# Four Strassen sets by turns with classical pairs in the down projection, and the last products added in DRAM by DMAs

## The chip, the cores and the metric

The kernel runs on one core of a Trainium2 chip. The metric is the device time of one execution in microseconds (us); for the kernel before, three runs gave 1673.4, 1674.53 and 1674.97 us, median 1674.53.

The engines are named as in the profile: PE (TensorE matmuls), PEld (TensorE weight loads), DVE (VectorE), ACT (ScalarE), POOL (GpSimd) and SP (SyncE). SP and POOL start most DMAs here.

## The reference

A decoder layer on 256 tokens of width 2048 in float32: a feed-forward half step, a mixer (attention beside a convolution), and a second feed-forward half step, each followed by a LayerNorm. The change lies in the down projection of the two feed-forward steps:

```python
def swiglu_ffn(x, w_gate, w_up, w_down):
    h = jax.nn.silu(x @ w_gate) * (x @ w_up)      # 256 x 5632
    return h @ w_down                             # 256 x 2048
x = layer_norm(ALPHA * x + 0.5 * swiglu_ffn(x, ...), ln_g, ln_b)
```

## The kernel before

**Two-term numbers.** Every float32 operand is split into a high part `hi` (a cast on ACT, L170) and a low part `lo` (raw minus `hi`, on DVE, L174). A product is three matmuls, hi·hi, hi·lo and lo·hi (`mm3`, L677 to L679), accumulated in PSUM.

**Parts.** The 5632 hidden features are worked in three parts, of 16, 16 and 12 blocks of 128. For each part the up projection comes first, then gate and transpose (the transposed tile goes out to DRAM and back by POOL's DMAs, L1044 and L1046), then the down projection of that part. Parts 0 and 1 project down to all 2048 columns, in two column pairs of 2 × 512 columns; their results are written or added into a DRAM tile `y` (`side`) by POOL's DMAs. Part 2 does its first two column chunks in the same way into SBUF and the rest otherwise. The two feed-forward steps so have eight column pairs that go to DRAM: four stretches ("downs") of two.

**Sets and pairs.** `by_sums` (L865) forms a 2 × 2 block product (two token halves by two column chunks) over K pairs of 256 features each. `KINDS` (L26) says for each K pair whether it is done classically ("C": 8 products, 24 matmuls, 2 weight tiles of 128 × 1024) or as a Strassen set ("S": 7 products, 21 matmuls). A set takes four weight sources out of the same two tiles `more`: DVE forms sums of them (L188, four subtractions), and the raw and summed tiles are each split. A set also needs sums of the four `hh` blocks on the left side, made when `hf` comes back (`split`, L1056).

**The eight banks.** All eight PSUM banks hold sums of one column pair: banks 1, 5, 6 and 7 of the Strassen products alone, banks 2, 4, 3 and 0 of products that belong to one output each. After the last set, `shared` (L941) combines banks 1, 5, 6 and 7 into four SBUF tiles `part` (one ACT copy, L944, and four DVE additions, L938). After the last classical pair, `leave` (L952) adds each of the banks 2, 4, 3, 0 to its `part` (DVE, L938), and POOL starts a DMA that writes `part` to `y` (L964, part 0 of the first step) or adds it there (`accum_op`, L962). The next column pair uses the same banks again, in the order 1, 5, 6, 7, 2, 4, 3.

**The order of the work** is the program's order: each engine has one queue, and takes its instructions in that order. `Steps` decides while the program is written when a weight source is split: `pace` (L279) puts in a split when its estimate of DVE's backlog is under `AHEAD` (1.2 us), at most `LEAD` (7) sources ahead of the one in use; during the last products of a column pair (`ending`) it puts in none. `hi` and `lo` have 8 buffers each, the raw tiles 4, the sets' tiles room for two sets. The tiles `part` (and others) take turns in 5 buffers of tag `z`: a new tile waits until all readers of the buffer's last tile are done, a DMA that reads it included.

Of the kernel before, what the change touches and what calls it, by code (L numbers as in the profile page):

```python
# [9 lines left out]
F32 = mybir.dt.float32  # L10
# [4 lines left out]
ALU = mybir.AluOpType  # L15
# [3 lines left out]
P = 128  # L19
# [3 lines left out]
KT = D // P  # L23
JT = DFF // P
PARTS = ((0, 16), (16, 32), (32, 44))
KINDS = ("SCCSCSCC", "SCCSCSCC", "SCCSCC")  # L26
BLOCKS = {"S": 7, "C": 4, "L": 8}
UP = (
# [35 lines left out]
ZB = 5  # L64
# [15 lines left out]
def blocks_of(columns):  # L80
    return lambda kind: BLOCKS["L" if kind == "S" and columns < NC_ else kind]
# [265 lines left out]
def hybrid_layer(  # L347
# [3 lines left out]
    nc = tc.nc  # L351
# [4 lines left out]
    act = ctx.enter_context(tc.tile_pool(name="act", bufs=1))  # L356
# [20 lines left out]
    def add_ffn(wu, wd, plain):  # L377
        for (j0, j1), kinds in zip(PARTS, KINDS):
            for g in range(j0 // JG, j1 // JG, 2):
                if g < plain:  # L380
                    sources.extend(wu[g + i, q, h] for i in range(2) for q in range(4) for h in range(2))
                else:
                    for t, kind in UP[up_of(g, j0, plain)]:
                        add_set(kind, [wu[g + i, t // 2, t % 2] for i in range(2)])
            for c in range(0, NC_, 2):
                if c > 0 and j1 == JT:
                    sources.extend(wd[c + i, t // 2, t % 2] for i in range(2) for t in range(j0 // 2, j1 // 2))
                    continue
                for t, kind in enumerate(kinds, j0 // 2):
                    add_set(kind, [wd[c + i, t // 2, t % 2] for i in range(2)])  # L390
# [290 lines left out]
    def block(x_, k, b):  # L681

        if x_.shape[2] == S:
            return x_[:, k, b * P : (b + 1) * P]
        kinds = KINDS[-1]
        return x_[:, sum(4 if y == "C" else 8 for y in kinds[: k // 2]) + 2 * (k % 2) + b]
# [235 lines left out]
    def down_by_sums(hh, hl, kinds, factor, side, more, columns, last):  # L922

        firsts = [sum(map(blocks_of(columns), kinds[:t])) for t in range(len(kinds))]
        places = {
            "S": ("21", "11", "22", "12", "S1", "S2", "S3", "S4")[-blocks_of(columns)("S"):],
            "C": ("21", "11", "22", "12"),
        }

        def blocks(t, name):  # L930
            n = firsts[t] + places[kinds[t]].index(name)
            return hh[:, n], hl[:, n]

        for c in range(0, columns, 2):
            tmp, places_ = [], {(0, 0): 0, (0, 1): 2, (1, 0): 1, (1, 1): 3}

            def add(out, ps, other):
                nc.vector.scalar_tensor_tensor(out=out, in0=ps, scalar=factor, in1=other, op0=ALU.mult, op1=ALU.add)  # L938
                st.vector(0.62, 0.3)

            def shared(bank, tmp=tmp):  # L941

                tmp.extend(act.tile([P, 512], F32, tag="z", name="part", bufs=ZB) for k in range(4))
                nc.scalar.mul(tmp[0], bank[1], factor)  # L944
                add(tmp[1], bank[6], tmp[0])
                add(tmp[2], bank[5], tmp[1])
                add(tmp[1], bank[7], tmp[1])
                add(tmp[3], bank[5], tmp[1])
                if last is not None:
                    last()  # L950

            def leave(at, ps, c=c, tmp=tmp):  # L952

                t = tmp[places_[at]]
                add(t, ps, t)
                if columns < NC_:
                    y = xts[0][:, 1 - at[0], (c + at[1]) * 512 : (c + at[1] + 1) * 512]
                    joins[1 - at[0], at[1]] = lambda: nc.vector.tensor_tensor(out=y, in0=y, in1=t, op=ALU.add)
                    return
                place = side[1 - at[0], :, (c + at[1]) * 512 : (c + at[1] + 1) * 512]  # L960
                if more:
                    nc.gpsimd.dma_start(place, t, accum_op=ALU.add)  # L962
                else:
                    nc.gpsimd.dma_start(place, t)  # L964

            by_sums(kinds, blocks, leave, shared)

    def ffn(xc, tag, skew, begun, prepare, finish, places, kept=None):
        with tc.tile_pool(name=f"ffn{tag}", bufs=2) as pool:
# [40 lines left out]

            for part, ((j0, j1), kinds) in enumerate(zip(PARTS, KINDS)):
                n = j1 - j0
# [108 lines left out]
                while g < j1 // JG:  # L1121
# [4 lines left out]
                    g += 2  # L1126
                side = sides[xc is not xcat]
                down_by_sums(
                    hh, hl, kinds, 0.5, side, part > 0 or xc is not xcat, columns, (lambda: tokens_back(side)) if ends else None
                )  # L1130
# [466 lines left out]
```

## Time and profile before

| what | value |
|---|---|
| median of three runs | 1674.53 us (1673.4 to 1674.97) |
| time of the profiled execution | 1675.41 us |
| its span, first to last instruction | 1673.6 us |
| DVE, ACT, POOL busy over the span | 1444.1 us (86%), 944.6 us (56%), 323.0 us (19%) |
| share of the DMA engines' time, SP's queue q1 and POOL's queue q0 | 56.6% and 11.1% |
| first and last matmul of the first down (stretch A) | 175.71 and 258.44 us |
| first matmul of the other downs (B, C, D) | 426.63, 1137.03 and 1387.95 us |

A row of the timeline has start, duration (of a merged run of equal instructions, "x4"), engine, line, operation, output from inputs, and in brackets the idle time before it and what ended that. A row of the windows has, for a stretch, its length and each engine's busy time (with its count of instructions), the granted TensorE clock, the share of the DMA engines and GB/s. A row of the groups has count, busy time and mean ns of one.

### The profile page before, as it was taken

Reading aid. Unit: us, or ns where it says so; the run is one execution under the profiler, and the core shown is the slowest. Engines: PE = TensorE matmul, PEld = TensorE weight load, DVE = VectorE, ACT = ScalarE, POOL = GpSimd, SP = SyncE. Lnnn points to the kernel's source line nnn. Section 1 sums busy time; section 2 is a strip of 40 time slices with the busy share of each in tenths; the row PEclk is TensorE's granted clock in tenths of the full one; section 3 lists DMA queues with packets and bytes.
Section 4 is the critical chain, followed back from the end, with each engine's and each line's share of the span. In section 5 each row is a group of like instructions: output and inputs, shape, how many; then the busy total and the mean of one; then the engine's idle time right before and its main releaser. Section 6 shows DMA issues by size and latency. Waiting matters only on the chain. (4 is left out here: it accounts for less than half of the span.)

```text
span 1673.6 us, 21985 instructions
## 1 busy us (share of the span) xinstructions
PE 1657.9 (99%) x7647; PEld 1375.4 (82%) x7647; DVE 1444.1 (86%) x2151; ACT 944.6 (56%) x1316; POOL 323.0 (19%) x302
## 2 busy tenths in 40 slices
PE   9999999999999999999999999999999999999997
PEld 7888888888878888888888888888888888888885
DVE  7899899888999987958888768799999888999877
ACT  6555555555555554676665466455555555556552
POOL 0100000111100001178996201000000000000012
PEclk9999999999999999999999999999999999999999
DMA  8667677677788666656654568666776666776665
GB/s 296 242 227 239 208 250 244 201 249 243 245 242 261 207 225 243 211 189 189 201 176 159 192 226 286 233 223 226 240 244 222 223 222 208 257 235 216 219 238 158
DMA packets 110976, 377.32 MB, mean 225 GB/s; under 512 B 13968, under 2 KB 14096, under 8 KB 110736
## 3 DMA queue, kind: packets, MB, share of 16 engines
q1 hardware_dynamic: 94032, 329.50, 56.6%
q0 software_dynamic: 16112, 45.10, 11.1%
q10 hardware_dynamic: 720, 1.31, 0.2%
q8 instruction: 60, 0.98, 0.2%
q14 instruction: 52, 0.43, 0.1%
HBM read 349.64 MB, written 27.26 MB: 225 GB/s over the span
## 5 line engine op out<-in xcount | busy, mean ns | idle before, releaser
L174 DVE TENSOR_TENSOR lo<-raw,hi 128x1024 fp32r<-128x1024 f32 x320 | 376.1, 1219 | 60.1 <-ACT hi L170 59.9
L677 PE MATMUL sum<-hi,xcat 128*128 128x512 f32 x1006 | 391.6, 389 | 0.4 <-DVE part L1077 0.4
L678 PE MATMUL sum<-lo,xcat 128*128 128x512 f32 x1006 | 391.4, 389 | 0.0
L679 PE MATMUL sum<-hi,xcat 128*128 128x512 f32 x1006 | 391.4, 389 | 0.0
L170 ACT CAST hi<-raw 128x1024 fp32r<-128x1024 f32 x320 | 321.5, 1047 | 59.2 <-DMA raw<-in_wd 19.0
L170 ACT CAST hi<-more 128x1024 fp32r<-128x1024 f32 (+1 forms) x210 | 190.6, 907 | 178.8 <-DVE more L188 158.7
L174 DVE TENSOR_TENSOR lo<-more,hi 128x1024 fp32r<-128x1024 f32 (+1 forms) x210 | 213.7, 1040 | 20.3 <-ACT hi L170 20.2
L677 PE MATMUL sum<-hi,hh 128*128 128x512 f32 x580 | 226.2, 390 | 1.3 <-DVE part L938 1.0
L678 PE MATMUL sum<-lo,hh 128*128 128x512 f32 x580 | 225.7, 389 | 0.0
L679 PE MATMUL sum<-hi,hl 128*128 128x512 f32 x580 | 225.7, 389 | 0.0
L677 PEld LDWEIGHTS sum<-hi,xcat 128*128 128x128 f32 x1006 | 188.8, 188 | 40.4 <-DVE part L1077 1.2
L679 PEld LDWEIGHTS sum<-hi,xcat 128*128 128x128 f32 x1006 | 188.8, 188 | 39.4
L678 PEld LDWEIGHTS sum<-lo,xcat 128*128 128x128 f32 x1006 | 188.8, 188 | 39.0
L253 ACT CAST hi<-raw 128x1024 fp32r<-128x1024 f32 (+1 forms) x156 | 158.5, 1029 | 93.2 <-PE acc L679 42.2
L256 POOL TENSOR_TENSOR lo<-raw,hi 128x1024 fp32r<-128x1024 f32 x73 | 175.9, 2436 | 111.6 <-ACT hi L253 104.8
L170 ACT CAST hi<-sum 128x512 fp32r<-128x512 f32 x140 | 86.8, 622 | 191.4 <-DVE sum L188 177.8
L1044 POOL DMA_DIRECT2D far<-hr x88 | 49.2, 564 | 753.0 <-DVE hr L1039 753.0
L677 PEld LDWEIGHTS sum<-hi,hh 128*128 128x128 f32 x580 | 108.8, 188 | 25.8 <-ACT hi L170 1.3
L679 PEld LDWEIGHTS sum<-hi,hl 128*128 128x128 f32 x580 | 108.9, 188 | 22.7
L678 PEld LDWEIGHTS sum<-lo,hh 128*128 128x128 f32 x580 | 108.9, 188 | 22.6 <-DVE lo L174 0.2
L1077 DVE TENSOR_TENSOR part<-sum,part 128x512 f32<-128x512 f32 x152 | 101.0, 687 | 26.8 <-PE sum L679 19.4
L256 DVE TENSOR_TENSOR lo<-raw,hi 128x1024 fp32r<-128x1024 f32 (+1 forms) x83 | 97.7, 1198 | 25.7 <-ACT hi L253 25.5
(210 smaller groups left out, 2436.1 us busy)
## 6 DMA issues: line engine op xcount, KB each, us to landing
raw<-in_wu SPq DMA_DIRECT2D x264, 512.0 KB, 5.0
raw<-in_wd SPq DMA_DIRECT2D x120, 512.0 KB, 5.3
more<-in_wu SPq DMA_DIRECT2D x84, 512.0 KB, 7.0
more<-in_wd SPq DMA_DIRECT2D x56, 512.0 KB, 7.3
raw<-in_win SPq DMA_DIRECT2D x52, 512.0 KB, 3.9
raw<-in_wout SPq DMA_DIRECT2D x32, 512.0 KB, 4.0
far<-hr POOLq DMA_DIRECT2D x88, 128.0 KB, 2.7
hf<-far POOLq DMA_DIRECT2D x22, 512.0 KB, 3.6
```

The source lines that it names most:

```text
L170: self.nc.scalar.copy(hi, x_)
L174: self.nc.vector.tensor_tensor(out=lo, in0=x_, in1=hi.bitcast(F32), op=ALU.subtract)
L253: nc.scalar.copy(hi, raw)
L256: eng.tensor_tensor(out=lo, in0=raw, in1=hi.bitcast(F32), op=ALU.subtract)
L677: nc.tensor.matmul(ps, s_hi, m_hi, start=start, stop=False)
L678: nc.tensor.matmul(ps, s_hi, m_lo, start=False, stop=False)
L679: nc.tensor.matmul(ps, s_lo, m_hi, start=False, stop=stop)
L1044: nc.gpsimd.dma_start(far[:, :, t].rearrange("f r n -> r f n"), hr[32 * t : 32 * t + 32])
L1077: nc.vector.tensor_tensor(out=out, in0=ps, in1=other, op=ALU.add)
```

## The change

Three things are changed.

1. `KINDS` of parts 0 and 1: from "SCCSCSCC" (three sets, five classical pairs) to "SCSCSCSC" (four and four). The last set is now followed by one classical pair, not two. Part 2 stays.
2. For the eight column pairs that go to DRAM, `shared` itself sends off the four `part` tiles (`write`), right after they are made.
3. `leave` no longer adds on DVE for these. ACT copies the bank, times `factor`, into a new tile `rest` of tag `z` (L972 of the new file), and POOL's DMA adds that to `y`. Each column pair so has eight DMAs of 256 KB to `y`, not four.

```diff
-KINDS = ("SCCSCSCC", "SCCSCSCC", "SCCSCC")
+KINDS = ("SCSCSCSC", "SCSCSCSC", "SCCSCC")
...
                 if last is not None:
                     last()
+                else:
+                    for at, k in places_.items():
+                        write(at, tmp[k], more)
+
+            def write(at, t, adds, c=c):
+
+                place = side[1 - at[0], :, (c + at[1]) * 512 : (c + at[1] + 1) * 512]
+                if adds:
+                    nc.gpsimd.dma_start(place, t, accum_op=ALU.add)
+                else:
+                    nc.gpsimd.dma_start(place, t)
 
             def leave(at, ps, c=c, tmp=tmp):
 
                 t = tmp[places_[at]]
-                add(t, ps, t)
                 if columns < NC_:
+                    add(t, ps, t)
...
-                place = side[1 - at[0], :, (c + at[1]) * 512 : (c + at[1] + 1) * 512]
-                if more:
-                    nc.gpsimd.dma_start(place, t, accum_op=ALU.add)
-                else:
-                    nc.gpsimd.dma_start(place, t)
+                t = act.tile([P, 512], F32, tag="z", name="rest", bufs=ZB)
+                nc.scalar.mul(t, ps, factor)
+                write(at, t, True)
```

The first place is ACT's queue around the end of the first column pair of stretch A, in the kernel before. The number behind `hi` is the weight source: sources 76 to 97 belong to this column pair, 98 to 101 are the first set of the next one. A name in "waits" is what the instruction waits for (DMAHW: a DMA of SP's queue, DMASW: one of POOL's).

```order
L170 CAST hi97_1856<-raw97_1746 128x1024 [waits DMAHW0_49,PE_49,Activation_49]
L170 CAST hi98_1877<-more_446 128x1024 [waits DMAHW1_49,PE_49,Activation_49]
L170 CAST hi99_1884<-sum99_1880 128x512 [waits DVE_49,PE_49]
L170 CAST hi99_1884<-sum99_1881 128x512 [waits DVE_49]
L944 ACTIVATE part_1892<-sum_1621 128x512
L170 CAST hi100_1917<-more_446 128x1024 [waits DVE_49,DMAHW2_49,PE_49,Activation_49]
L170 CAST hi101_1929<-more_446 128x512 [waits DVE_49,PE_49]
L170 CAST hi102_1942<-raw102_1830 128x1024 [waits DMAHW3_49,PE_49,Activation_49]
```

The same place in the changed kernel. Here the column pair has sources 76 to 99, its last set is 94 to 97 and its last classical pair 98 and 99; 100 to 103 are the first set of the next column pair.

```order
L170 CAST hi101_1916<-sum101_1913 128x512 [waits DVE_49]
L170 CAST hi102_1939<-more_446 128x1024 [waits DVE_49,DMAHW2_49,PE_49,Activation_49]
L944 ACTIVATE part_1943<-sum_1623 128x512
L972 ACTIVATE rest_1962<-sum_1626 128x512 [waits PE_49]
L972 ACTIVATE rest_1971<-sum_1627 128x512 [waits DMASW4_49,DVE_49,PE_49]
L972 ACTIVATE rest_1986<-sum_1628 128x512 [waits DMASW5_49,DVE_49,PE_49]
L972 ACTIVATE rest_1989<-sum_1628 128x512 [waits DMASW6_49,DVE_49]
L170 CAST hi103_2002<-more_446 128x512 [waits DVE_49]
L170 CAST hi104_2005<-raw104_1818 128x1024 [waits DMAHW3_49]
L170 CAST hi105_2012<-raw105_1827 128x1024 [waits DMAHW4_49]
```

The four copies `rest` stand in one row ahead of the cast of source 103. The first takes the one free buffer of tag `z`; the second, third and fourth each wait for a DMA of POOL's queue. At the end of the second column pair of each down the rows stand in the same way, with all four sources of the following set cast ahead of the copies.

POOL's queue there, in the changed kernel (L961 writes, L959 adds):

```order
L961 DMA y0_137<-part_1943 128x512 [waits Activation_49]
L961 DMA y0_137<-part_1945 128x512 [waits DVE_49]
L961 DMA y0_137<-part_1944 128x512 [waits DMASW6_49,DVE_49]
L961 DMA y0_137<-part_1946 128x512 [waits DVE_49]
L959 DMA y0_137<-rest_1962 128x512 [waits DMASW4_49,Activation_49]
L959 DMA y0_137<-rest_1971 128x512 [waits DMASW6_49,Activation_49]
L959 DMA y0_137<-rest_1986 128x512 [waits DMASW5_49,Activation_49]
L959 DMA y0_137<-rest_1989 128x512 [waits DMASW7_49,DMASW3_49,Activation_49]
```

Each addition of a `rest` waits for the DMA of the `part` that goes to the same place: DMASW4, 5 and 6 are raised by the first, second and third of these rows. The copies of ACT that wait for DMASW4, 5 and 6 so wait until these three DMAs have landed. In the kernel before there were four DMAs here, each after its `leave`.

DVE's queue around `shared`, in the changed kernel:

```order
L174 TENSOR_TENSOR lo100_1901<-more_446,hi100_1900 128x1024 [waits Activation_49]
L174 TENSOR_TENSOR lo101_1917<-sum101_1912,hi101_1916 128x512 [waits Activation_49]
L174 TENSOR_TENSOR lo101_1917<-sum101_1913,hi101_1916 128x512 [waits Activation_49]
L188 TENSOR_TENSOR more_446<-more_446 128x512
L174 TENSOR_TENSOR lo102_1940<-more_446,hi102_1939 128x1024 [waits Activation_49]
L938 SCALAR_TENSOR_TENSOR part_1944<-sum_1625,part_1943 128x512 [waits PE_49,Activation_49]
L938 SCALAR_TENSOR_TENSOR part_1945<-sum_1625,part_1944 128x512 [waits DVE_49]
L938 SCALAR_TENSOR_TENSOR part_1944<-sum_1624,part_1944 128x512 [waits DVE_49,PE_49]
L938 SCALAR_TENSOR_TENSOR part_1946<-sum_1625,part_1944 128x512 [waits DVE_49]
L188 TENSOR_TENSOR more_446<-more_446,sum101_1913 128x512
L174 TENSOR_TENSOR lo103_2003<-more_446,hi103_2002 128x512 [waits PE_49,Activation_49]
L174 TENSOR_TENSOR lo104_2006<-raw104_1818,hi104_2005 128x1024 [waits DMAHW3_49,PE_49,Activation_49]
```

Ahead of the four additions stand the low parts up to source 102; before, they stood up to source 98. The low part of 103, and all behind it, needs a cast that stands behind the four copies on ACT.

## Prediction

> **What bounds the kernel now.** I read the page first, then who waits for whom, then the two column pairs of the first down (stretch A) by windows, and then the engines' timelines at the end of a column pair.
>
> ```profile
> PE 1657.9 (99%) x7647; PEld 1375.4 (82%) x7647; DVE 1444.1 (86%) x2151; ACT 944.6 (56%) x1316; POOL 323.0 (19%) x302
> PE sum L677 <- DVE part L938: 1.0, 2, 0.9
> 175.71:217.20 41.49, 41.49 (x185) 34.36 (x184) 37.22 (x49) 22.75 (x30) 2.77 (x5) 1.00 0.60 207
> 217.20:258.70 41.50, 41.50 (x185) 34.37 (x184) 38.77 (x48) 23.48 (x28) 2.75 (x5) 1.00 0.66 232
> ```
>
> PE is never idle in a column pair of A, so a matmul less is time less. The longest entry of PE's waits in the downs is 1.0 us in all, for the additions that the change removes. But DVE is close behind: 37.2 and 38.8 us busy in 41.5. ACT has room, 23 of 41.5. So DVE has some 3 us of slack per column pair, and the change must be weighed on DVE, and on whatever keeps DVE from working.
>
> **PE: what is saved.** The first and last matmul of A:
>
> ```profile
> 175.71 0.39 PE L677 MATMUL sum<-hi,hh 128*128 128x512 f32 x1
> 258.44 0.39 PE L679 MATMUL sum<-hi,hl 128*128 128x512 f32 x1
> ```
>
> A has two column pairs of 3×21 + 5×24 = 183 matmuls, 366 in all: 82.73 / 365 = 0.2267 us each. One set in place of a classical pair saves 3 matmuls; eight column pairs save 24, **5.4 us**. A column pair then has 180 matmuls, 40.8 us. A set takes 4.76 us, a classical pair 5.44.
>
> **DVE: what is added.** One set and the two classical sources after it:
>
> ```profile
> 183.53 0.65 DVE L188 TENSOR_TENSOR sum<-more 128x512 f32<-128x512 f32 x1
> 184.21 0.69 DVE L188 TENSOR_TENSOR sum<-more,sum 128x512 f32<-128x512 f32 x1
> 184.82 0.68 DVE L188 TENSOR_TENSOR more<-more 128x512 f32<-128x512 f32 x1
> 185.43 1.22 DVE L174 TENSOR_TENSOR lo<-more,hi 128x1024 fp32r<-128x1024 f32 x1
> 186.68 0.69 DVE L188 TENSOR_TENSOR more<-more,sum 128x512 f32<-128x512 f32 x1
> 187.29 1.28 DVE L174 TENSOR_TENSOR lo<-sum,hi 128x512 fp32r<-128x512 f32 x2
> 188.49 1.82 DVE L174 TENSOR_TENSOR lo<-more,hi 128x1024 fp32r<-128x1024 f32 x2
> 190.23 2.35 DVE L174 TENSOR_TENSOR lo<-raw,hi 128x1024 fp32r<-128x1024 f32 x2
> 192.50 0.68 DVE L188 TENSOR_TENSOR sum<-more 128x512 f32<-128x512 f32 x1
> ```
>
> From start to start a set costs DVE 190.23 − 183.53 = 6.70 us and a classical pair 192.50 − 190.23 = 2.27. The swap adds 4.43. The four additions of `leave` go; at about 0.6 us from start to start, like the 512-wide rows above, that is 2.4. Net +2.0 us per column pair on DVE while PE's share falls by 0.7: slack of about 3 us becomes about none. ACT gets three casts of 512 more (a set has two of 1024 and three of 512, a classical pair two of 1024) and four copies of 0.59, 4.2 us in all; it is idle for 18 us of a column pair, so in time that has room. POOL gets four issues more, some 3.5 us beside its 2.8 of 41.5, and its next other work after a down is the transpose of the next part, tens of us later. What matters is where ACT's copies stand.
>
> **ACT: the wait that is added.** `shared` in A, on ACT and DVE, with what DVE does just ahead of it:
>
> ```profile
> 209.35 0.59 ACT L944 ACTIVATE part<-sum 128x512 f32<-128x512 f32 x1
> 248.55 0.59 ACT L944 ACTIVATE part<-sum 128x512 f32<-128x512 f32 x1
> 207.37 0.68 DVE L188 TENSOR_TENSOR sum<-more 128x512 f32<-128x512 f32 x1
> 208.09 0.69 DVE L188 TENSOR_TENSOR sum<-more,sum 128x512 f32<-128x512 f32 x1
> 208.70 1.22 DVE L174 TENSOR_TENSOR lo<-more,hi 128x1024 fp32r<-128x1024 f32 x1
> 209.97 2.94 DVE L938 SCALAR_TENSOR_TENSOR part<-sum,part 128x512 f32<-128x512 f32 x4
> ```
>
> A DMA to `y` in stretch B, from its addition on, then the landing times of the 24 adding DMAs (L962) and of the 8 plain ones (L964, in A):
>
> ```profile
> 471.12 0.68 DVE L938 SCALAR_TENSOR_TENSOR part<-sum,part 128x512 f32<-128x512 f32 x1
> 472.24 0.88 POOL L962 DMA_DIRECT2D y<-part  x1 [11.56 <-DVE part L938]
> DMA to landing us min/median/max: 5.2/7.6/9.8
> DMA to landing us min/median/max: 3.4/5.5/7.0
> ```
>
> Of the four new copies, the second to fourth wait for the first three of these DMAs to land, and behind the fourth stand ACT's casts for the next sources. Let T be the start of the copy L944. The third addition of `shared` ends about T+2.8 (0.62 to the first, three of some 0.73). POOL issues the first DMA at T+1.0, the second at T+2.5, the third 0.88 later, T+3.4. With the median of 7.6 the third lands at T+11.0; the fourth copy, 0.59, ends at **T+11.6**. For the plain ones of A, with 5.5 and an issue at T+3.1, it is T+9.2. Casts and low parts then follow at these times:
>
> ```profile
> L170 ACT CAST hi<-more 128x512 fp32r<-128x512 f32 x70 | 43.5, 622 | 70.8 <-DVE more L188 70.8
> L174 DVE TENSOR_TENSOR lo<-more,hi 128x512 fp32r<-128x512 f32 x70 | 47.9, 685 | 7.8 <-ACT hi L170 7.8
> L170 ACT CAST hi<-raw 128x1024 fp32r<-128x1024 f32 x320 | 321.5, 1047 | 59.2 <-DMA raw<-in_wd 19.0 <-DMA raw<-in_wu 17.8 <-ACT hi L170 12.2
> L174 DVE TENSOR_TENSOR lo<-raw,hi 128x1024 fp32r<-128x1024 f32 x320 | 376.1, 1219 | 60.1 <-ACT hi L170 59.9
> ```
>
> After the first column pair of a down the next source is 103: 0.62 + 0.69, ready at T+12.9 (A: 10.5). PE comes to it one classical pair and five products of the next set after its last set's end E: 5.44 + 15×0.2267 = E+8.84. After the second column pair the whole next set is ready, and the next source is classical: 1.05 + 1.22, T+13.9 (A: 11.5), wanted at E + 5.44 + 4.76 = E+10.20. With the lag T − E, PE stands still for lag + 4.1 and lag + 3.7 us (A: lag + 1.7 and + 1.3).
>
> The lag now: E is 135 matmuls, 30.60 us, after a column pair's start, so 209.35 − 206.31 = 3.0 us, and 248.55 − 247.80 = 0.75 in the second. In the changed kernel DVE has, from the start of the down to `shared`, one set more and one classical pair less (+4.4), and it has got to source 102, not 98: 5.5 us of the next set (two subtractions, one 1024-wide and two 512-wide low parts, a subtraction, a 1024-wide one) for the 2.5 of the rows above. That is +7.4, and E comes 21 matmuls later, 4.8: the lag becomes 3.0 + 7.4 − 4.8 = **5.6**. So the first stall is 9.7 us (A: 7.3). For the second: T to T takes DVE 39.2 now (209.35 to 248.55), 41.2 with the 2.0 added, and DVE lies idle behind ACT from its last addition and one subtraction, T+4.2, to the end of the cast, T+12.2, 8.0 us (A: 5.6). PE takes 40.8 and the first stall. Lag: 5.6 + 41.2 + 8.0 − 40.8 − 9.7 = 4.3 (A: 5.6 + 41.2 + 5.6 − 40.8 − 7.3 = 4.3), stall 8.0 (A: 5.6).
>
> **The sum.** Three downs at 17.7 and A at 12.9: 66.0 us of stalls. Less 5.4 for matmuls and 1.0 for the wait that goes: +59.6 on the profiled execution's 1675.41, 1735.0; that execution was 0.9 over the median, so the forecast is **1734 us**.
>
> Bounds of the unknown sizes. Lag 0.75 everywhere and the shortest landings (5.2 and 3.4, that is 2.4 and 2.1 off): stalls 2.45 + 2.05 per down in B, C and D, 0.35 in A, 14 in all, net +7, 1682. Longest landings (9.8, 7.0) with the lags above: 2.2 more per stall in three downs, 1.5 in A, +16, net +76, 1750. Not in the sum: the left side's sums for a further set, once per down, of this kind:
>
> ```profile
> L1001 DVE TENSOR_TENSOR sums<-hf 128x128 f32<-128x128 f32 x32 | 7.8, 283 | 0.0
> ```
>
> Four of 0.28 add 1.1 to the first lag of a down, 4 in all. And DVE leaves each down with no lead over PE, which the up projections before had to spare at will; a stall or two of some 3 us in each of the four that follow would add some 8 to 12, which makes 1762 of the 1750. I take the medians: 24 and 8 DMAs of the same kind, size and place.
>
> **The rivals.**
>
> *The landing is short.* While ACT waits, raw tiles aren't freed and SP loads nothing, so the DMA engines, at 0.60 to 0.70 now, may be free for these DMAs. With the shortest landing seen, 3.4, for all: third landing T+6.8, copy T+7.4, source 103 at T+8.7. Stalls lag − 0.1 = 5.5 and, with DVE's idle time 3.8, lag 5.6 + 41.2 + 3.8 − 40.8 − 5.5 = 4.3, 4.3 − 0.5 = 3.8: 9.3 a down, 37, net +31, 1705. Against it: all 24 adding DMAs took 5.2 or more, with the load as it was. [...]
>
> *DVE alone is the bound.* If the copies wait for nothing late, what is left is DVE's lag of 5.6: bank 5 is free at T+3.6 and wanted at E + 5.44 + 0.68, a stall of 3.1, then about 0.5 in the second: 14 in all, net +8, 1682. It needs landings under 3 us.
>
> *Faster.* DVE sheds 32 additions of 512 from the ends of the column pairs, where PE's only waits were, and ACT is idle for 18 us of each. If the copies are hidden, only the 5.4 and 1.0 are left: −6.4, 1668. It decides at the landing: with the smallest lag, 0.75, source 103 is in time if the third DMA lands 2.8 us after its issue (8.84 − 0.75 − 3.4 − 0.59 − 0.62 − 0.69). Of 32 DMAs none did. [...]
>
> *Not what it says.* The rows show 24 matmuls fewer, 32 additions fewer and 32 copies more; I give nothing to this.
>
> **Chances.** Forecast 0.79 (its own range 1695 to 1762); short landing 0.10 (1695 to 1715); DVE alone 0.05 (1677 to 1690); faster 0.06. A measurement of this kernel can tell about 0.2%, 3.3 us, from no change. Slower by more than that: 0.91, since of the second and third case some 0.03 ends within it; same 0.03; faster 0.06. The range for 8 in 10 leaves out the two last cases and a part of the forecast's ends: 1695 to 1762.
>
> **What would show it.** Right: on ACT, L972 idle before it with DMA `y<-part` as what ended the wait, three times per column pair; PE waiting at the first set of the next column pair for ACT or DVE (`hi`, `lo`, `rest`, `part`), 5 to 10 us each time, eight times; DVE idle some 6 to 8 us behind L170 at these places; PE busy time down by about 5 us. Wrong: PE's windows in the downs still full, or idle time in them with no L972 ahead of it; or PE waiting in the up projections instead.

## The result, and the profile after

The changed kernel takes 1744.58 us (median of four runs, 1743.28 to 1745.0); the kernel before, on the same chip, 1673.97 us. The ratio is 1.0421, interval 1.0405 to 1.0437: **4.2% slower**, 70.6 us. The profiled execution has a span of 1743.1 us, 69.5 more than the one of before.

The page's first part, then PE's and ACT's waits that bear on the downs (whole execution: total us, times, longest), and the two column pairs of A, the first up to the next one's first matmul, the second to the end of its last, in the changed kernel:

```profile
PE 1686.0 (97%) x7623; PEld 1387.7 (80%) x7623; DVE 1466.2 (84%) x2195; ACT 978.2 (56%) x1376; POOL 350.5 (20%) x334
PE sum L677 <- DVE part L938: 17.9, 8, 2.7
PE sum L677 <- ACT part L944: 8.4, 8, 2.9
PE sum L677 <- ACT hi L170: 7.6, 3, 3.4
PE sum L678 <- DVE lo L174: 6.5, 9, 1.3
PE sum L677 <- ACT rest L972: 4.1, 3, 1.9
ACT rest L972 <- DMA y<-part: 56.7, 24, 5.0
175.46:217.96 42.50, 41.27 (x181) 33.52 (x179) 38.24 (x54) 23.27 (x32) 2.77 (x5) 1.00 0.54 191
217.96:264.87 46.91, 44.25 (x180) 35.74 (x180) 39.43 (x50) 25.21 (x32) 5.76 (x8) 0.93 0.75 224
```

There are 24 matmuls fewer, and PE is busy 28.1 us longer. The second window tells why: the granted clock is 0.93 there. Who waits is also not what one would guess from ACT's 56.7 us of waiting for landings: PE's two longest entries, 26.3 us together, name the additions L938 and the copy L944 of `shared`, which wait for no landing themselves. PE's timeline at the end of the first column pair of A shows how these lie:

```profile
217.18 0.39 PE L679 MATMUL sum<-hi,hl 128*128 128x512 f32 x1
217.96 0.50 PE L677 MATMUL sum<-hi,hh 128*128 128x512 f32 x1 [0.39 <-ACT part L944]
...
218.54 0.39 PE L679 MATMUL sum<-hi,hl 128*128 128x512 f32 x1
221.58 0.80 PE L677 MATMUL sum<-hi,hh 128*128 128x512 f32 x1 [2.65 <-DVE part L938]
...
222.60 0.63 PE L679 MATMUL sum<-hi,hl 128*128 128x512 f32 x1
...
227.96 0.39 PE L677 MATMUL sum<-hi,hh 128*128 128x512 f32 x1
```

PE stops at the first product of the next column pair (bank 1), three matmuls later at the second (bank 5), and then runs for some 6 us with 0.43 us from start to start where 0.227 is its pace; the granted clock from 221.58 to 227.60 is 0.50. ACT and DVE in the same place:

```profile
216.37 1.05 ACT L170 CAST hi<-more 128x1024 fp32r<-128x1024 f32 x1 [2.44 <-DVE more L188]
217.32 0.59 ACT L944 ACTIVATE part<-sum 128x512 f32<-128x512 f32 x1
217.81 0.59 ACT L972 ACTIVATE rest<-sum 128x512 f32<-128x512 f32 x1
221.09 0.60 ACT L972 ACTIVATE rest<-sum 128x512 f32<-128x512 f32 x1 [2.69 <-DMA y<-part]
223.25 0.60 ACT L972 ACTIVATE rest<-sum 128x512 f32<-128x512 f32 x1 [1.57 <-DMA y<-part]
224.37 0.60 ACT L972 ACTIVATE rest<-sum 128x512 f32<-128x512 f32 x1 [0.52 <-DMA y<-part]
```

```profile
217.45 1.23 DVE L174 TENSOR_TENSOR lo<-more,hi 128x1024 fp32r<-128x1024 f32 x1 [1.25 <-ACT hi L170]
218.59 2.93 DVE L938 SCALAR_TENSOR_TENSOR part<-sum,part 128x512 f32<-128x512 f32 x4
...
225.50 0.69 DVE L174 TENSOR_TENSOR lo<-more,hi 128x512 fp32r<-128x512 f32 x1 [3.38 <-ACT hi L170]
```

The three waits for landings are there, with ACT's casts behind them and DVE idle for 3.38 us; but PE's stop at bank 5 ends at 221.58, with DVE's four additions, before any of that reaches PE.

I counted PE's starts against its pace of 0.227 from start to start, over all products of the projections (tile `sum`). Stops with a named wait cost 50.8 us, in 31 places (before: 2.0, in 3). Matmuls at half clock, which start 0.38 to 0.46 after the one before, cost 21.3 us, and there are 107 (before: none). Other starts more than 0.30 after the one before cost 7.1 (before: 2.3). Less 5.4 us for the 24 matmuls that is +69.5, all of the span's growth. The same count comes within 1.4 us of the span's growth in every run below.

### The profile page after: what moved, and what is told of

It is laid out like the page before. It is cut to its first block, busy times and chain, and to the rows that moved or that the text cites. A ratio compares the mean times of both kernels' runs of the same rounds, so it can differ in the third digit from the quotient of the medians.

```text
span 1743.1 us, 22118 instructions
## 1 busy us (share of the span) xinstructions
PE 1686.0 (97%) x7623; PEld 1387.7 (80%) x7623; DVE 1466.2 (84%) x2195; ACT 978.2 (56%) x1376; POOL 350.5 (20%) x334
## 3 DMA queue, kind: packets, MB, share of 16 engines
q0 software_dynamic: 20720, 53.49, 14.3%
## 5 line engine op out<-in xcount | busy, mean ns | idle before, releaser
L174 DVE TENSOR_TENSOR lo<-raw,hi 128x1024 fp32r<-128x1024 f32 x304 | 357.5, 1220 | 74.1 <-ACT hi L170 74.1
L170 ACT CAST hi<-raw 128x1024 fp32r<-128x1024 f32 x304 | 306.7, 1047 | 53.8 <-DMA raw<-in_wu 21.9
L170 ACT CAST hi<-more 128x1024 fp32r<-128x1024 f32 (+1 forms) x234 | 212.3, 907 | 187.3 <-DVE more L188 166.6
L174 DVE TENSOR_TENSOR lo<-more,hi 128x1024 fp32r<-128x1024 f32 (+1 forms) x234 | 239.0, 1042 | 54.5 <-ACT hi L170 54.0
L677 PE MATMUL sum<-hi,hh 128*128 128x512 f32 x572 | 228.8, 400 | 19.7 <-DVE part L938 10.6
L170 ACT CAST hi<-sum 128x512 fp32r<-128x512 f32 x156 | 96.3, 622 | 168.3 <-DVE sum L188 162.3
L1086 DVE TENSOR_TENSOR part<-sum,part 128x512 f32<-128x512 f32 x152 | 101.0, 687 | 26.3 <-PE sum L679 18.4
```

Source lines behind the costliest of these rows:

```text
L170: self.nc.scalar.copy(hi, x_)
L174: self.nc.vector.tensor_tensor(out=lo, in0=x_, in1=hi.bitcast(F32), op=ALU.subtract)
L677: nc.tensor.matmul(ps, s_hi, m_hi, start=start, stop=False)
L1086: nc.vector.tensor_tensor(out=out, in0=ps, in1=other, op=ALU.add)
```

## The experiments

Two theories went into them. **W**: the copies' wait for landings parks ACT's casts, and that is most of the loss (the forecast's sum). **L**: with only one classical pair after the last set, `shared` comes too late for banks 1 and 5, and the half clock follows. The kernel before took 1675.07 us beside the first four runs, 1674.03 beside the next four and 1673.78 beside the last four; each ratio goes by its own.

**The parts of the change alone.** The kernel before with the four sets only:

```diff
-KINDS = ("SCCSCSCC", "SCCSCSCC", "SCCSCC")
+KINDS = ("SCSCSCSC", "SCSCSCSC", "SCCSCC")
```

> The kernel before with SCSCSCSC alone: the last additions stay on DVE, no ACT copies. Theory W (the copies' wait for DMA landings parks ACT's casts and is most of the loss): that wait is not there, so what is left is 24 matmuls less and a late bank 5: 1675 to 1690 us. Theory L (the last set is followed by one classical pair only, DVE comes to shared 5 to 7 us after the set's end, banks 1 and 5 are free too late, and the clock halves after the stop): DVE has 2.4 us more per column pair than in the changed kernel, 1715 to 1750 us.

Measured: **1704.9 us**, ratio 1.0172 (1.0157 to 1.0187), between the two ranges. And the changed kernel with the sets of before, that is, the copies and DMAs only:

```diff
-KINDS = ("SCSCSCSC", "SCSCSCSC", "SCCSCC")
+KINDS = ("SCCSCSCC", "SCCSCSCC", "SCCSCC")
```

> The changed kernel with the old SCCSCSCC: copies on ACT and additions in DRAM, but two classical pairs behind the last set. Theory W: three copies still wait for landings with casts behind them, a stall of about lag + 1, 2 to 5 us in each of eight column pairs: 1690 to 1710 us. Theory L: shared is in time as before, the casts in time too: 1668 to 1677 us.

Measured: **1678.67 us**, ratio 1.0026 (1.0014 to 1.0039), a little over L's range. The parts alone cost 30 and 4 us, together 70.6: the other 37 come only when both are there.

**The wait taken away.** The changed kernel with the copies in buffers of a tag that no DMA of the `part` tiles holds:

```diff
-                t = act.tile([P, 512], F32, tag="z", name="rest", bufs=ZB)
+                t = act.tile([P, 512], F32, tag="bc", name="rest", bufs=BC)
```

> The changed kernel with the copies rest in buffers of tag bc (6), which are free: none waits for a landing of its own column pair. Theory W: about 1682 us (the stalls of a late bank 5, 14, less 6). Theory L: PE still stands at banks 1 and 5, some 3.5 us and a half clock after it of some 2.7, at eight ends: 1710 to 1735 us.

Measured: **1710.95 us**, ratio 1.0203 (1.0184 to 1.0223). The edit is worth 33.6 us, half of the loss; W, which gave the wait nearly all, falls. Two of PE's waits in this kernel, then PE and DVE at the end of A's first column pair, and PE at the end of the second:

```profile
PE sum L677 <- ACT part L944: 15.2, 8, 4.2
PE sum L677 <- ACT rest L972: 5.8, 8, 1.0
```

```profile
220.21 0.50 PE L677 MATMUL sum<-hi,hh 128*128 128x512 f32 x1 [0.97 <-ACT rest L972]
```

```profile
218.90 2.93 DVE L938 SCALAR_TENSOR_TENSOR part<-sum,part 128x512 f32<-128x512 f32 x4
```

```profile
261.10 0.39 PE L679 MATMUL sum<-hi,hl 128*128 128x512 f32 x1
264.37 0.80 PE L677 MATMUL sum<-hi,xcat 128*128 128x512 f32 x1 [2.88 <-ACT part L944]
```

No copy waits for a DMA, and PE still stands for the copy of bank 1, at the ends of the second column pairs longer than with the wait (2.9 to 4.2 us; with the wait 0.6 to 2.9); the half clock follows (behind 264.37, the starts from 266.91 to 271.17 are 0.42 or 0.43 us apart).

The edit did more than end the wait. The second product of the next column pair now waits for the copies L972 at all eight ends, and not for the additions L938. In A it starts at 220.21, while the additions, two of which read bank 5, run until 221.83: so it goes to another bank, and the next column pair does not use the same banks in the same order here. The additions L938 cost PE 17.9 us in the changed kernel and nothing here, the copies L972 4.1 there and 5.8 here. And 14.3 of the 33.6 us are half clock (35 matmuls at it, not 107). How much of the 33.6 is the wait for landings alone, no run shows.

**Two classical pairs last.** The changed kernel with another order of its four sets:

```diff
-KINDS = ("SCSCSCSC", "SCSCSCSC", "SCCSCC")
+KINDS = ("SSCSCSCC", "SSCSCSCC", "SCCSCC")
```

> The changed kernel with the four sets in the order SSCSCSCC, so two classical pairs follow the last set; copies and their waits as in the changed kernel. Theory W: the wait for landings stays, 1700 to 1735 us. Theory L: bank 5 is wanted 5.4 us later, its stall goes: 1668 to 1690 us.

Measured: **1693.78 us**, ratio 1.011 (1.0087 to 1.0132), between the two ranges. Then this order and the other buffers at once (both diffs above):

> The changed kernel with two edits at once: the copies of the last four banks take buffers of another tag, so that they wait for no landing, and the four sets stand SSCSCSCC, so that two classical pairs follow the last set. If the wait for landings and the place of the last set are the two losses and nothing else is, both are gone and what is left is the saving of 24 matmuls less small waits: 1666 to 1678 us. If a fourth set is too much for VectorE wherever it stands (its backlog at the two sets in a row), some 5 to 15 us stay: 1680 to 1692.

Measured: **1693.71 us**, ratio 1.0115 (1.0102 to 1.0129), a little over the second range. Equal: in this order the wait for landings costs nothing. In the first of the two, ACT's wait for landings and PE's two longest entries are

```profile
ACT rest L972 <- DMA y<-part: 1.4, 3, 0.6
PE sum L678 <- DVE lo L174: 8.6, 9, 2.1
PE sum L677 <- ACT rest L972: 6.7, 6, 1.4
```

The `part` tiles go off a classical pair earlier there, and have landed when the last banks are ready, but for the three waits of 1.4 us in all. Some 20 us are left, at other places: PE waits for low parts at the first classical pair behind the two sets that now begin a down (0.5 to 2.1 us) and at the third set (0.8), and in the next column pair for the copies of the last banks, up to 1.4 us at a time. In stretch B of the second run DVE does the transpose's work (L1034, L1048) ahead of two low parts, and PE stands for these, with the half clock behind it (the starts from 443.75 to 446.74 are 0.42 or 0.43 us apart):

```profile
439.39 1.43 DVE L1034 TENSOR_TENSOR ht<-part 128x256 f32<-128x256 f32 x4
440.85 1.25 DVE L1048 STREAM_TRANSPOSE hr<-ht 128x1024 f32<-128x1024 f32 x1
442.02 2.32 DVE L174 TENSOR_TENSOR lo<-raw,hi 128x1024 fp32r<-128x1024 f32 x2
```

```profile
443.26 0.69 PE L678 MATMUL sum<-lo,hh 128*128 128x512 f32 x1 [2.06 <-DVE lo L174]
```

**Copies and DMAs without the wait**, with the sets of before (the diff of the buffers, and the sets as in the second run above):

> The changed kernel with the sets of before (three, two classical pairs last) and copies that wait for no landing: only the additions moved from VectorE to ScalarE's copies and the DMAs are left of the change. If the landing wait was all that this part cost, the half-clocked stop in stretch B of the run with these sets goes too, and the time is at or a little below the kernel before: 1670 to 1676 us. If eight DMAs in place of four, or the copies' place ahead of the casts, cost something of their own, it stays at 1677 to 1681.

Measured: **1673.35 us**, ratio 0.9995 (0.9985 to 1.0004): no difference to the kernel before, and 5.3 us under the run with the wait. (One of its eleven executions took 4147 us, which nothing here explains; the ratio does not count it.) DVE is busy 16.0 us less than before, and it buys nothing:

```profile
PE 1656.1 (99%) x7647; PEld 1376.9 (82%) x7647; DVE 1428.1 (86%) x2119; ACT 958.9 (57%) x1348; POOL 350.5 (21%) x334
```

**The number of sets, or the place of the last.** The kernel before, its additions and DMAs kept, with four sets and two classical pairs last:

```diff
-KINDS = ("SCCSCSCC", "SCCSCSCC", "SCCSCC")
+KINDS = ("SSCSCSCC", "SSCSCSCC", "SCCSCC")
```

> The kernel before with four sets as SSCSCSCC; its additions on VectorE and its four DMAs stay. Theory 'place': the loss of the four sets alone (1705 us with one classical pair after the last set) comes from where the last set stands, so with two pairs after it most of it goes: 1668 to 1682 us. Theory 'number': VectorE's work for a fourth set, 4.4 us more per column pair with the four additions kept, is the loss wherever the set stands: 1692 to 1710.

Measured: **1703.28 us**, ratio 1.0175 (1.0161 to 1.0188). And with its three sets, the last one place later:

```diff
-KINDS = ("SCCSCSCC", "SCCSCSCC", "SCCSCC")
+KINDS = ("SCCSCCSC", "SCCSCCSC", "SCCSCC")
```

> The kernel before with its three sets, the last of them moved by one place (SCCSCCSC), so that one classical pair follows it and not two. No product, no split and no DMA is added or removed. Theory 'place': the additions of the last set's banks come too late for the next column pair's first products, banks 1 and 5, in all eight column pairs, as with four sets: 1695 to 1715 us. Theory 'number': with three sets VectorE has its slack and the order does not matter: 1672 to 1680.

Measured: **1701.38 us**, ratio 1.0155 (1.0141 to 1.0169). Moving one set by one place, with not an instruction more, costs 27 us, nearly as much as the four sets alone. But theory "place" is not the whole: the four sets with two pairs last, begun with two sets in a row, cost as much. PE's waits of the three-set run are at the same two banks, but only at the ends of the four first column pairs; theory "place" had them at all eight. ACT and DVE at the end of A's first column pair:

```profile
PE sum L677 <- DVE part L938: 7.8, 4, 2.0
PE sum L677 <- ACT part L944: 7.1, 4, 3.2
```

```profile
175.95 0.39 PE L677 MATMUL sum<-hi,hh 128*128 128x512 f32 x1
...
209.57 0.69 DVE L188 TENSOR_TENSOR sum<-more 128x512 f32<-128x512 f32 x1
...
215.17 1.23 DVE L174 TENSOR_TENSOR lo<-more,hi 128x1024 fp32r<-128x1024 f32 x1 [1.25 <-ACT hi L170]
...
217.61 0.59 ACT L944 ACTIVATE part<-sum 128x512 f32<-128x512 f32 x1
218.23 4.14 DVE L938 SCALAR_TENSOR_TENSOR part<-sum,part 128x512 f32<-128x512 f32 x6 [1.24 <-ACT part L944]
```

The last set ends 159 matmuls after 175.95, at 212.0; the copy starts at 217.61, a lag of 5.6 us with three sets. Ahead of the additions DVE is at the next column pair's first set from 209.57 to 218.23, 8.7 us, 2.5 of them waiting for ACT. `pace` splits up to seven sources ahead of the one in use. Four of the seven were sources of the two classical pairs behind the last set, two are now, so more of them belong to the next set; before, what stood there took 2.5 us. PE wants bank 1 one classical pair, 5.44 us, after the last set, and not 10.88.

The same three-set order with the copies and DMAs of the changed kernel, waiting for landings:

```diff
-KINDS = ("SCSCSCSC", "SCSCSCSC", "SCCSCC")
+KINDS = ("SCCSCCSC", "SCCSCCSC", "SCCSCC")
```

> The changed kernel, copies that wait for landings included, with three sets as SCCSCCSC: one classical pair after the last set, as in the changed kernel, but no fourth set. If the wait for landings costs its 34 us wherever one classical pair follows the last set (with two it costs 0 to 5 in the runs so far), this is 1701, the time with this order and VectorE's additions, plus 25 to 40: 1725 to 1742 us. If the wait costs that much only on top of the fourth set's work on VectorE, 1700 to 1715.

Measured: **1729.1 us**, ratio 1.0337 (1.0313 to 1.0361). And with the copies in the other buffers as well:

> As the last one (SCCSCCSC, additions by DMAs), but the copies wait for no landing. If the place of the last set is a loss of its own, 25 to 30 us over the kernel before, whatever adds the last banks: 1695 to 1706 us. If VectorE's additions at the end of the column pair were what made it late there, taking them away gives most of it back: 1676 to 1690.

Measured: **1697.8 us**, ratio 1.0154 (1.0134 to 1.0173). The edit of the buffers is worth 31.3 us here, about as with four sets: it goes with the place of the last set, not with the fourth set. Here too the second product waits for the copies, and not for L938, at the ends of the first column pairs. ACT's waiting for landings in the first of the two is a little less than in the changed kernel:

```profile
ACT rest L972 <- DMA y<-part: 48.0, 22, 4.9
```

**Four sets, better placed**, copies in the other buffers, two classical pairs last. First the two neighbouring sets at the end:

```diff
-KINDS = ("SCSCSCSC", "SCSCSCSC", "SCCSCC")
+KINDS = ("SCSCSSCC", "SCSCSSCC", "SCCSCC")
```

> Four sets with two classical pairs last, no wait for landings, but the two sets that stand side by side are the third and fourth, not the first two as in the run of 1694 us, where TensorE stood for low parts at the second set of a column pair and the halved clock followed once. If VectorE is late only because a down begins with two sets in a row, this recovers 10 to 25 us: 1668 to 1684. If two sets in a row cost the same at any place, or bring the last set's additions late again: 1690 to 1710.

Measured: **1683.03 us**, ratio 1.0057 (1.0042 to 1.0072). Then in the middle:

```diff
-KINDS = ("SCSCSCSC", "SCSCSCSC", "SCCSCC")
+KINDS = ("SCSSCSCC", "SCSSCSCC", "SCCSCC")
```

> As the last one with the two neighbouring sets as the second and third of the four (SCSSCSCC). If a run-up of one classical pair is enough for VectorE's lead, 1668 to 1684 us, and if the stops only move to the third set and the additions behind the last, 1690 to 1710.

Measured: **1680.34 us**, ratio 1.004 (1.0025 to 1.0055). This is the best with four sets, 64 us under the changed kernel and still 0.4% over the kernel before. PE waits for one thing in its downs, low parts at the two neighbouring sets, mostly the second:

```profile
PE sum L678 <- DVE lo L174: 8.1, 12, 1.4
```

All of them in one table (medians, us):

| sets, classical pairs behind the last | additions on DVE | copies and DMAs, waiting | copies and DMAs, no wait |
|---|---|---|---|
| 3, two (SCCSCSCC) | 1674 (before) | 1678.7 | 1673.4 |
| 3, one (SCCSCCSC) | 1701.4 | 1729.1 | 1697.8 |
| 4, one (SCSCSCSC) | 1704.9 | 1744.6 (after) | 1711.0 |
| 4, two (SSCSCSCC) | 1703.3 | 1693.8 | 1693.7 |
| 4, two (SCSCSSCC) | | | 1683.0 |
| 4, two (SCSSCSCC) | | | 1680.3 |

Down the first column, the place of the last set costs 27.4, and the fourth set there 3.5 more. Along the rows, taking the wait away is worth 31.3 and 33.6 with one classical pair last, the other bank included, and 5.3 and 0.1 with two. (The kernel before took up to 1.3 us more or less beside the runs compared.) No version tried beats the kernel before by more than the measurement can tell.

## Why the prediction was right, and where its working was not

Direction and size came out: 1744.6 us, 10.6 over the forecast, inside the range. That it came so near is in part luck: the stalls were forecast 12 us too high, and 21.3 us of half clock were not in the sum. By its steps:

- **The 24 matmuls.** They are gone (7647 to 7623), 5.4 us. That PE's busy time would fall by about 5 us was wrong: it rose by 28.1, mostly for the half clock, which the forecast didn't have.
- **The first lag, 5.6.** In A the last set ends 156 matmuls and one stop of 1.0 us after 175.46, at 211.8, and L944 starts at 217.32: 5.5. The number was right, its working in part: it counted a fourth set and the work on the next set, and the run with three sets, the last one late, has the same 5.6 without a fourth.
- **The second lag, 4.3.** In A the down's last matmul starts at 264.48, so its last set ended at 264.48 + 0.23 − 5.44 = 259.3, and L944 stands at 266.11: 6.8, where 4.3 was forecast. From T to T it was 48.8 us, not 46.8. The missing term is seen in DVE's rows at a set in the second column pair, here of the run whose copies don't wait:

```profile
244.27 0.69 DVE L188 TENSOR_TENSOR sum<-more 128x512 f32<-128x512 f32 x1
...
249.88 1.23 DVE L174 TENSOR_TENSOR lo<-more,hi 128x1024 fp32r<-128x1024 f32 x1 [1.25 <-ACT hi L170]
...
252.45 0.69 DVE L174 TENSOR_TENSOR lo<-more,hi 128x512 fp32r<-128x512 f32 x1 [0.74 <-ACT hi L170]
253.41 2.36 DVE L174 TENSOR_TENSOR lo<-raw,hi 128x1024 fp32r<-128x1024 f32 x2 [0.27 <-ACT hi L170]
255.68 0.69 DVE L188 TENSOR_TENSOR sum<-more 128x512 f32<-128x512 f32 x1
```

A set and a classical pair take 11.4 us here, as in the changed kernel (246.67 to 258.07), not 6.70 + 2.27: subtraction, cast and low part wait for one another by turns (1.25 + 0.74 + 0.27 on DVE). The price of 6.70 came from a place where such waits were covered by other work.

- **The waits for landings.** L972 stood for `y<-part` 24 times, three per column pair, as said. The fourth copy ended at T+7.7 and T+7.2 in A (forecast 9.2) and at T+10.2 to T+11.8 in the others (11.6). The shorter ones of A are the plain DMAs:

```profile
DMA to landing us min/median/max: 2.7/2.9/4.7
```

- **The sum of 66.0 us of stalls.** This step is the one that was mis-sized, and its cause was too simple. PE's stops and late starts grew by 50.8 + 7.1 − 2.0 − 2.3 = 53.6 us, 12 fewer than forecast, and 21.3 us of half clock, priced nowhere, came on top. The sign "5 to 10 us each time, eight times" did not come: the named stops at an end add up to 3.0 to 6.9 us, under 5 at four of the eight, and in A, where 7.3 and 5.6 were forecast, no cast stopped PE (3.0 and 3.9, all for L944 and L938). The stalls also have two causes, one inside the other: PE stops first at banks 1 and 5, which no landing holds up, and only then for casts parked behind the copies. The sum took the later end of the two, and so named the landing as the cause of all; the edit that takes the wait away gives back 33.6 us, with the second product in another bank.
- **The rival "DVE alone", 1682 us.** The run without the wait comes nearest to it, 1710.95. It priced the first stall at 3.1 and the second at 0.5. The 3.1 is what A's first stall for banks 1 and 5 is in the changed kernel (0.39 + 2.65). Without the wait, and with the other bank, the first was 0.37 + 0.97 us and the second 2.88 + 0.30, because the second lag is long: 264.37 is 8.5 us after that set's end at 261.10 + 0.23 − 5.44 = 255.9. Half clock after it (35 matmuls in all, 7.0 us) is the rest of the error that I can name.
- **"Faster" and the offload to ScalarE.** Without the wait and with the sets of before, the additions moved off DVE bring 0.9995: neither gain nor loss. The move frees DVE of 16.0 us; PE was the bound (busy 99% of the span in both), and in the kernel before it waited 1.0 us in all for those additions.

What stays open: how much of the 33.6 us the wait for landings is and how much the other bank; whether `shared` placed ahead of the next set's splits on DVE would make one classical pair enough, which was not tried; and why the fourth set costs 3.5 us with DVE's additions but 13 to 16 with the copies, in the same place.

## What to carry to other kernels

A change in a table that sets an order also moves whatever is tied to its entries: count, for each step tied to the moved one, what now stands ahead of it in its engine's queue and when the next user wants its buffer. Where two waits lie one inside the other, price each as if the other were gone; the outer one hides the inner, and taking it away gave back less here than was put down to it: 33.6 us, the other bank included, of 66.0 forecast. And a unit price read where other work covers the waits did not hold where DVE had lost its lead: 8.97 us by the price for a set and a classical pair, 11.4 measured.

## What the runs showed of the hardware

The half clock after short stops was not expected. PE's rows in one kernel, the last but one, whose third and fourth set are neighbours, in A and in D:

```profile
202.39 0.50 PE L678 MATMUL sum<-lo,hh 128*128 128x512 f32 x1 [1.70 <-DVE lo L174]
...
203.72 0.50 PE L678 MATMUL sum<-lo,hh 128*128 128x512 f32 x1 [0.37 <-DVE lo L174]
204.05 0.39 PE L679 MATMUL sum<-hi,hl 128*128 128x512 f32 x1
...
1418.99 0.50 PE L678 MATMUL sum<-lo,hh 128*128 128x512 f32 x1 [1.62 <-DVE lo L174]
...
1420.31 0.58 PE L678 MATMUL sum<-lo,hh 128*128 128x512 f32 x1 [0.37 <-DVE lo L174]
1420.69 0.63 PE L679 MATMUL sum<-hi,hl 128*128 128x512 f32 x1
```

Much the same pair of stops has full pace behind it in A and half of it in D: the starts from 204.05 to 204.98 are 0.23 or 0.24 us apart, those from 1420.69 to 1423.68 0.42 or 0.43. In the run with the four sets alone, a stop of 2.64 us at bank 5 has five half-clock matmuls behind it in A (222.76 to 224.47, each 0.42 or 0.43 after the one before) and none in D (stop before 1455.01, then 0.23 to 0.24 us apart up to 1457.68, but for the first, 0.34). So the length of a stop alone did not decide in these runs, and a stop of 1.62 us, with one of 0.37 soon behind it, had the half clock after it. What decided, no run shows.
